# First stage of an encoder layer on one core: root sums over 128 columns, two whole and three shared early steps, the first two products by turns

## The chip, the cores and the metric

The kernel runs on one core of a Trainium2 chip. Its time is the device time of one execution, in microseconds (us). A core has five engines with a queue of instructions each: TensorE (PE in the profile; PEld is its loading of the stationary operand), VectorE (DVE), ScalarE (ACT), GpSimd (POOL) and SyncE (SP), which here only issues transfers. Each engine takes its own instructions in the order in which they stand. Data in DRAM come and go by DMA, issued on SyncE's queue or on GpSimd's.

## The reference

One layer of an encoder: 1024 tokens, width 1024. It is computed in float32.

```python
h = h + 0.5 * swiglu(rms_norm(h, ffn1_norm[l]), ffn1_w_gate[l], ffn1_w_up[l], ffn1_w_down[l])
u = rms_norm(h, mix_norm[l])
z = u @ w_in[l]
...
merged = jax.nn.sigmoid(ga) * (ya @ w_branch_a[l]) + jax.nn.sigmoid(gb) * (yb @ w_branch_b[l])
h = h + merged @ w_out[l]
h = h + 0.5 * swiglu(rms_norm(h, ffn2_norm[l]), ffn2_w_gate[l], ffn2_w_up[l], ffn2_w_down[l])
...
def rms_norm(x, g):
    xf = x.astype(jnp.float32)
    y = xf * lax.rsqrt(jnp.mean(xf * xf, axis=-1, keepdims=True) + EPS)
    return (y * g.astype(jnp.float32)).astype(x.dtype)

def swiglu(x, w_gate, w_up, w_down):
    return (jax.nn.silu(x @ w_gate) * (x @ w_up)) @ w_down
```

Between the projection `z` and `merged` stand two attentions, which the change does not touch. The feed-forward width is 2816.

## The kernel before

**Products.** Every large matrix product is done by a scheme of Strassen's kind: each operand is cut into four quadrants, and seven products of half-size operands (named P1, P2, P5, P6, P3, P7, P4, in this order) stand for eight. Each operand is split into a high and a low part (`split`, lines 86 to 89: a cast on ScalarE, a subtraction on VectorE), and `mm3` (lines 137 to 144) multiplies high by high, high by low and low by high. One product of a weight tile of 128 columns with 512 tokens is four steps of three matmuls, 128 x 128 by 128 x 512: twelve matmuls.

**The first stage**, the gate and up products of the first feed-forward, works through pairs `i` of weight tiles, 11 of them; `m` is 0 for gate and 1 for up, so a pair has 14 products. The right operands are seven combinations of the quadrants of x (transposed, tokens in the columns): B11, B21, T1, T2, B22, T3, T4 for the products P1, P2, P5, P6, P3, P7, P4. They are made on ScalarE and VectorE while TensorE works. B11 and B21 need only the first half of the tokens and the gain; T1 and all later ones need, for the second half, the ratio of the roots of the norm of the two halves. So P1 and P2 of the first five pairs are done ahead ("early", 20 products), while the sums of squares of the two halves are formed (`square`) and their roots taken (`roots`): four matmuls of the summed squares with a column of ones, the mean and the power on GpSimd, and `spread`, which lays a root out over the partitions by VectorE multiplications and four transposes. With `hidden` the first root is applied to the results just before the gate's Silu, by `units`.

**Shared and whole pairs.** In a "merged" (here: shared) pair, P1 is copied out of its PSUM bank to a buffer `u`, P2 is added to it in the bank, which gives the first quadrant, and `u` is later added to P5, P6 and P4 by VectorE. In a whole pair, P1 stays in its bank, where P6, P7 and P4 are accumulated on it, and is copied out after P1 and after P6; no `u` is needed, but the bank is held. Before the change all five early pairs are shared. Their `u` go to DRAM (`u1_d`, `store_u`, GpSimd's queue) and come back with the first quadrant when the pair's turn comes (`load_u`, SyncE's queue).

**Order.** `products` builds the list `seq` of products, `prep(q)` loads and splits the weights of product q, `prep_until` says how many are prepared ahead, and `run` is a generator that gives one step of TensorE at a time; the code around it drains so many steps between the pieces of other work. A scheduler then sets the order on each engine, except for instructions in `pin(...)`. Weights are loaded to four buffers `raw` and to two that x itself occupies at first (`extra`, tiles 6 and 7 of `fa`); intermediate results of a pair go round a `ring` of buffers in `fx` and `fa`. The small pools are `hs` (four of 512 columns) and `xs` (two of 1024). The same functions do the gate and up products of the second feed-forward, and the projection `z`, with one shared pair (i = 2); there `late_homes` places `u` in the gain's buffer and the first quadrants of pairs 2 and on in `hs`.

The early order and the lookahead of the first stage are these lines:

```python
early = [(i, p, m) for i in sorted({0, 1, *merged}) for p in ("P1", "P2") for m in range(2)]
if spill:
    early[:8] = [(i, p, m) for p in ("P1", "P2") for i in range(2) for m in range(2)]
...
prep_until(q + 3 if q < len(early) - 4 else min(2 * q - len(early) + 7, q + 8))
```

## Time and profile before

| what | us |
| --- | --- |
| median of 3 runs | 1967.34 |
| lowest, highest | 1966.22, 3939.23 |
| the profiled execution | 1967.33 |
| its span, first to last instruction | 1965.2 |

The span is what the profile's page and views cover; the other 2.1 us of that execution lie around it. In the page, the busy time of an engine is the union of its instructions, so a full TensorE reads as busy even where its clock is low; the granted clock is a column of its own (1.00 is full). A row of the timeline has start, duration, engine, line, operation, tiles written and read, shapes, count, and in brackets the idle time before it and what ended it. Consecutive matmuls overlap in the rows: their pace is the distance of the starts.

### The profile page before, as it was taken

What the parts mean: (1) busy time and instruction counts of PE and PEld (TensorE: products, weight loads), DVE (VectorE), ACT (ScalarE), POOL (GpSimd) and SP (SyncE); (2) the same over time, 40 slices, a digit from 0 to 9 for tenths busy, and PEclk for the clock granted to TensorE, in tenths of its full rate; (3) what the DMA queues carried; (4) which work ended last, traced back from release to release, by engine and by line L of the source; (5) the groups of instructions that cost most, each with busy time, mean ns of one, the idle gap of its engine ahead of it and who ended that gap; (6) DMA issues with size and microseconds to landing.
All of it is one profiled execution on the core that took longest, in us unless ns stands there. A gap on an engine that the chain in (4) does not pass through costs nothing.

```text
span 1965.2 us, 25704 instructions
## 1 busy us (share of the span) xinstructions
PE 1928.7 (98%) x8928; PEld 1601.5 (81%) x8928; DVE 1477.3 (75%) x2622; ACT 940.8 (48%) x1823; POOL 343.5 (17%) x441
## 2 busy tenths in 40 slices
PE   8999999999999999999999999999999999999998
PEld 6778888888888777888888888887888888888886
DVE  7899776668957777678878857999766556569864
ACT  6433333334446543467777873366333333344453
POOL 2011010003400112311112134500101001005100
PEclk9999999999999999999999999999999999999999
DMA  8565333367333489983358675543433332493341
GB/s 256 174 193 162 102 104 111 108 242 266 97 107 125 134 220 222 187 214 92 96 141 183 182 230 205 181 139 113 150 96 108 107 103 97 146 356 98 108 144 59
DMA packets 273873, 302.63 MB, mean 154 GB/s; under 512 B 47792, under 2 KB 200752, under 8 KB 273744
## 3 DMA queue, kind: packets, MB, share of 16 engines
q1 hardware_dynamic: 216432, 212.80, 35.4%
q0 software_dynamic: 57312, 88.20, 16.2%
q8 instruction: 70, 1.15, 0.3%
q14 instruction: 59, 0.48, 0.1%
HBM read 211.72 MB, written 89.32 MB: 153 GB/s over the span
## 4 chain that ended last, share of the span: by engine, by line
PE 75%; issue 9%; DVE 7%; DMA 4%; POOL 2%; ACT 2%; SPq 0%; POOLq 0%; DVEq 0%; ACTq 0%
PE g L140 14%; PE g L142 14%; PE g L144 14%; PE d L144 9%; PE d L140 9%; PE d L142 9%; PE d L1261 2%; DVE ws L89 1%; POOL zs_d L872 1%; PE g L1275 1%; PE d L1241 1%; PE d L1240 1%; DMA raw<-zr_d 1%; PE g L1280 1%; DMA zs_d<-hs 1%
## 5 line engine op out<-in xcount | busy, mean ns | idle before, releaser
L140 PE MATMUL g<-ar,ws 128*128 128x512 f32 x1192 | 450.1, 399 | 17.7 <-ACT ar L716 6.1
L142 PE MATMUL g<-ar,ws 128*128 128x512 f32 x1192 | 443.1, 393 | 0.1
L144 PE MATMUL g<-ar,ws 128*128 128x512 f32 x1192 | 441.3, 392 | 0.0
L89 DVE TENSOR_TENSOR ws<-raw,ws 128x512 fp32r<-128x512 f32 (+1 forms) x339 | 244.3, 725 | 167.1 <-ACT ws L88 165.2
L88 ACT CAST ws<-raw 128x512 fp32r<-128x512 f32 (+1 forms) x341 | 215.0, 638 | 279.2 <-PE d L144 114.2
L140 PEld LDWEIGHTS g<-ar,ws 128*128 128x128 f32 x1192 | 220.3, 190 | 61.7 <-ACT ar L716 6.3
L142 PEld LDWEIGHTS g<-ar,ws 128*128 128x128 f32 x1192 | 225.4, 189 | 48.7 <-DVE ar L717 1.3
L144 PEld LDWEIGHTS g<-ar,ws 128*128 128x128 f32 x1192 | 225.5, 189 | 47.9
L140 PE MATMUL d<-ar,ws 128*128 128x512 f32 x672 | 260.0, 391 | 0.9 <-ACT ws L88 0.8
L144 PE MATMUL d<-ar,ws 128*128 128x512 f32 x672 | 259.6, 390 | 1.0 <-DVE ws L89 1.0
L142 PE MATMUL d<-ar,ws 128*128 128x512 f32 x672 | 259.4, 390 | 0.0
L144 PEld LDWEIGHTS d<-ar,ws 128*128 128x128 f32 x672 | 126.4, 188 | 28.3 <-DVE ws L89 1.9
L140 PEld LDWEIGHTS d<-ar,ws 128*128 128x128 f32 x672 | 126.4, 188 | 27.8 <-ACT ws L88 1.7
L142 PEld LDWEIGHTS d<-ar,ws 128*128 128x128 f32 x672 | 126.4, 188 | 26.3
L89 DVE TENSOR_TENSOR ws<-ar,ws 128x512 fp32r<-128x512 f32 x114 | 105.9, 936 | 7.0 <-ACT ws L88 7.0
L88 ACT CAST ar<-raw 128x512 fp32r<-128x512 f32 (+1 forms) x83 | 56.0, 679 | 89.9 <-PE g L142 47.7
L413 POOL DMA_DIRECT2D hid<-fx x89 | 48.1, 540 | 287.6 <-DVE fx L474 143.7
L140 PE MATMUL g<-ws,ws 128*128 128x512 f32 x232 | 91.0, 392 | 0.1
L142 PE MATMUL g<-ws,ws 128*128 128x512 f32 x232 | 90.4, 390 | 0.0
L144 PE MATMUL g<-ws,ws 128*128 128x512 f32 x232 | 90.4, 390 | 0.0
L1248 ACT ACTIVATE fa<-fa,nmx 128x385 f32<-128x385 f32 (+3 forms) x128 | 75.6, 591 | 25.8 <-DVE nmx L1245 25.0
L89 DVE TENSOR_TENSOR ws<-fa,ws 128x512 fp32r<-128x512 f32 x74 | 51.0, 690 | 46.9 <-ACT ws L88 46.5
(312 smaller groups left out, 3535.0 us busy)
## 6 DMA issues: line engine op xcount, KB each, us to landing
raw<-hid SPq DMA_DIRECT2D x70, 512.0 KB
hid<-fx POOLq DMA_DIRECT2D x89, 256.0 KB, 2.3
raw<-in_ffn_w_up_dram SPq DMA_DIRECT2D x35, 512.0 KB
ar<-in_ffn_w_down_dram SPq DMA_DIRECT2D x32, 512.0 KB
raw<-in_ffn_w_gate_dram SPq DMA_DIRECT2D x31, 512.0 KB
raw<-in_w_in_dram SPq DMA_DIRECT2D x27, 512.0 KB
ar<-zs_d POOLq DMA_DIRECT2D x48, 256.0 KB, 5.2
hid<-fa POOLq DMA_DIRECT2D x43, 256.0 KB, 2.3
```

Source lines behind the costliest of these rows:

```text
L88: nc.scalar.copy(dst_hi, src)
L89: (eng or nc.vector).tensor_tensor(dst_lo, src, f32v(dst_hi), op=ALU.subtract)
L140: nc.tensor.matmul(b, lhs[0], r[0], start=first, stop=False, **kw)
L142: nc.tensor.matmul(b, lhs[0], r[1], start=False, stop=False, **kw)
L144: nc.tensor.matmul(b, lhs[1], r[0], start=False, stop=last, **kw)
L413: nc.gpsimd.dma_start(hid[PRODUCTS.index(p), i], src)
L872: nc.gpsimd.dma_start(dst.rearrange("p b r w -> p b (r w)"), t.rearrange("p (b k) -> p b k", b=NTT))
L1240: nc.tensor.matmul(b[:, :nw], un["q"][s], un["kd"][s][:, k0 * P:k1 * P], start=True, stop=False)
L1241: nc.tensor.matmul(b[:, :nw], un["q"][s], un["kl"][s][:, k0 * P:k1 * P], start=False, stop=True)
L1248: nc.scalar.activation(pr, pr, AF.Exp, scale=-1.0, bias=nmx[:, s:s + 1], accum_out=ssum[:, s:s + 1])
L1261: nc.tensor.transpose(pt[:, i * P:(i + 1) * P], un["pr"][s][:, i * P:(i + 1) * P], ident)
L1275: nc.tensor.matmul(o[:, s], un["v"][s][:, un["k0"] + i, :], un["p"][s][:, i], start=i == 0, stop=i == last)
```

## The change

The first stage:

- The gain column `gcol` comes by GpSimd's queue and not as the first transfer of SyncE's. The first up weights come behind the first chunk of x.
- The first two products (gate and up of pair 0, P1) run by turns, one step each, so that every chunk of x serves both.
- Pairs 0 and 1 are whole, pairs 2, 3 and 4 shared. The `u` of pairs 2 and 3 stay in the two `xs` buffers, that of pair 4 in `hs`; nothing of them goes to DRAM. The first quadrant still comes back from `hid`, where it is stored anyway. The first quadrant's product P2 of pair 0, m = 0, leaves its bank one product late (`if spill and q == 4`), when the first root is there.
- The root: four matmuls of the summed squares with a 128 x 128 matrix of 1/1024, so that 128 equal columns come out; one addition, one power on four columns. `spread` transposes the root's columns broadcast to 128 columns, without multiplications. The sums and spreads stand later in the order of products.
- Weights are prepared three products ahead up to the 26th product of this stage, and up to eight from there on; before, the lookahead grew from the 17th on.

The other two stages with `products`: u and the first quadrant of pair 2 go to the gain's buffer and to one `xs` buffer, the first quadrants of pairs 3 and on to the ring. The second half of pair 0's weights is loaded with the first half and not during the transition.

```diff
         def home(i, key, m):
-            if i < 2:
+            if i != 2:
                 return None
             if (key, m) not in homes:
-                if key == "u":
-                    u = const.tile([P, 1152], F32, tag="gain", bufs=1, name=nm_("u"))
-                    homes["u", 0], homes["u", 1] = u[:, :512], u[:, 512:1024]
-                else:
-                    homes[key, m] = main.tile([P, 512], F32, tag="hs", bufs=4, name=nm_("hs"))
+                u = const.tile([P, 1152], F32, tag="gain", bufs=1, name=nm_("u"))
+                c = xs4()
+                for k in range(2):
+                    homes["u", k], homes["11", k] = u[:, k * 512:k * 512 + 512], c[:, k * 512:k * 512 + 512]
             return homes[key, m]
...
-                if (i, m, half) not in raws and not (half and q < 4):
+                if (i, m, half) not in raws :
                     load(i, m, half)
...
-                b = bks[i]["X", m] = bank("gd"[i % 2] if spill else "d")
+                b = bks[i]["X", m] = bank("d")
...
-                b = bks[i]["X", m] = bank("g" if i == 0 else "d")
+                b = bks[i]["X", m] = bank("g" if i == 0 and not spill else "d")
...
         def run():
+            slow = len(early) + (6 if spill else -4)
             for q in range(len(seq)):
-                prep_until(q + 3 if q < len(early) - 4 else min(2 * q - len(early) + 7, q + 8))
-                yield from multiply(q)
-                i, p, m = seq[q]
...
+                prep_until(q + 3 + min(max(q - slow, 0), 5))
+                if not spill or q > 1:
+                    yield from multiply(q)
+                elif q == 0:
+                    for _ in zip(multiply(0), multiply(1)):
+                        yield
+                if spill and q == 4:
+                    continue
+                for k in ((4, 5) if spill and q == 5 else (q,)):
+                    leave(k)
...
-                for m in range(2):
-                    load(0, m, 1)
...
-                if not whole:
+                if spill and i <= merged[-1]:
                     snap["11", 1] = None
+                elif not whole:
+                    snap["11", 1] = sn()
...
     gcol = const.tile([P, NC8], F32, name="gcol")
+    nc.gpsimd.dma_start(gcol, n1c)
...
+    mean = main.tile([P, 512], F32, tag="s1", bufs=1, name=nm_("s1"))[:, :P]
+    nc.gpsimd.memset(mean, 1.0 / D)
...
     def home_1(i, key, m):
-        return main.tile([P, 512], F32, tag="hs", bufs=4, name=nm_("hs")) if i < EARLY else None
...
+        if key == "u" and i < 4:
+            if m == 0:
+                late_u[i] = xs4()
+            return late_u[i][:, m * 512:m * 512 + 512]
+        return main.tile([P, 512], F32, tag="hs", bufs=4, name=nm_("hs")) if i < 5 else None
+
+    def load_11(i, snap, sn):
+        snap["11", 0] = sn()
+        nc.sync.dma_start(snap["11", 0], hid[PRODUCTS.index("P1"), i])
+
+    hg = hidden(wg1[0], wu1[0], down.at_end, (2, 3, 4), home_1, unit, load_11, (9, 11, 1, 3, 5, 7, 0, 2, 4, 6, 8, 10))
...
-    nc.sync.dma_start(gcol, n1c)
     hg[4](0, 0, 0)
-    for c in range(4):
+    load_xq(0, 0)
+    hg[4](0, 1, 0)
+    for c in range(1, 4):
         load_xq(c, 0)
...
-            pin(nc.tensor.matmul(b[:, j:j + 1], total[:, j * P:(j + 1) * P], ones, start=True, stop=True))
+            pin(nc.tensor.matmul(b[:, j * P:(j + 1) * P], total[:, j * P:(j + 1) * P], mean, start=True, stop=True))
...
-        pin(nc.vector.tensor_scalar(ms, b[:, :4], 1.0 / D, EPS, op0=ALU.mult, op1=ALU.add))
-        for j in range(4):
-            nc.gpsimd.tensor_tensor(r[:, j:j + 1], ms[:, j:j + 1], nhalf, op=ALU.pow)
+        pin(nc.vector.tensor_scalar_add(ms, b.rearrange("p (j t) -> p j t", j=4)[:, :, 0], EPS))
+        nc.gpsimd.tensor_tensor(r, ms, nhalf4, op=ALU.pow)
...
-            pin(nc.vector.tensor_scalar_mul(w[:, j * P:(j + 1) * P], spare, cols[:, j:j + 1]))
-        return w, b, dst
...
+            pin(nc.tensor.transpose(b[:, j * P:(j + 1) * P], cols[:, j:j + 1].broadcast_to([P, P]), ident))
         pin(nc.scalar.copy(dst, b))
...
     drain(run, 4)
     r = roots(0, total)
-    w = spread(units[:, :512], r)
+    drain(run, 4)
+    spread(units[:, :512], r)
...
-    drain(run, 4)
-    spread_end(*w)
-    unit["r"] = units[:, :512]
+    drain(run, 8)
     for c in range(4, 8):
         total = square(1, c)
+    hg[3](3, place=raw4)
     drain(run, 8)
     r = roots(1, total)
-    w = spread(units[:, 512:1024], r)
+    hg[3](4, place=raw4)
     drain(run, 4)
-    spread_end(*w)
-    hg[3](3, place=raw4)
+    spread(units[:, 512:1024], r)
...
-    chunks(T1, t1, 2, -1.0)
-    hg[3](4, place=raw4)
+    drain(run, 8)
+    chunks(T1, t1, 4, -1.0)
```

How the instructions stand now is shown at three places. First ScalarE at the start of the program, before; `ws` is a split weight tile, `raw` a loaded one, `fx` a chunk of x, `ar_79` the operand B11, `ar_117` the squares, and numbers tell buffers of one name apart:

```order
L88 CAST ws_128<-raw_92 128x512
L716 ACTIVATE ar_79<-fx_75,gcol 128x512
L716 ACTIVATE ar_79<-fx_76,gcol 128x512
L716 ACTIVATE ar_79<-fx_77,gcol 128x512
L716 ACTIVATE ar_79<-fx_78,gcol 128x512
L88 CAST ws_131<-raw_98 128x512
L88 CAST ws_134<-raw_100 128x512
```

And the same place on ScalarE now; line 725 is what was line 716:

```order
L88 CAST ws_127<-raw_93 128x512
L725 ACTIVATE ar_79<-fx_75,gcol 128x512
L725 ACTIVATE ar_79<-fx_76,gcol 128x512
L88 CAST ws_130<-raw_96 128x512
L725 ACTIVATE ar_79<-fx_77,gcol 128x512
L725 ACTIVATE ar_79<-fx_78,gcol 128x512
L88 CAST ws_133<-raw_101 128x512
```

The second weight tile has moved from behind the four chunks of x to a place behind the second.

Second, TensorE at the first root, before; `g` and `d` are PSUM banks, `ar_79` and `ar_80` the operands B11 and B21, `ar_117` holds the sum of squares:

```order
L142 MATMUL d_217<-ar_79,ws_160 128x512
L144 MATMUL d_217<-ar_79,ws_160 128x512
L140 MATMUL g_137<-ar_80,ws_187 128x512
L731 MATMUL d_230<-ones,ar_117 128x1 x4
L142 MATMUL g_137<-ar_80,ws_187 128x512
```

And now; `s_11_88` is the matrix of 1/1024, line 740 the sums:

```order
L142 MATMUL d_231<-ar_80,ws_176 128x512
L144 MATMUL d_231<-ar_80,ws_176 128x512
L740 MATMUL d_244<-s_11_88,ar_118 128x128 x4
L140 MATMUL d_256<-ar_80,ws_202 128x512
L142 MATMUL d_256<-ar_80,ws_202 128x512
```

The sums stood behind the first matmul of the fifth product and stand now behind its last, eleven matmuls later, with a whole product between them and the transposes.

Third, VectorE where pair 0 ends and the weights of the second pair's P5 are prepared, before; line 717 is the last piece of T4 (`ar_426`), lines 329, 335 and 336 form the sums of weight quadrants for P5, line 89 is the low part of a split, line 464 adds P3 or P7 to what is there, lines 407 to 474 are the gate and what follows it:

```order
L717 SCALAR_TENSOR_TENSOR ar_426<-fa,ar_426 128x512
L89 TENSOR_TENSOR ws_732<-raw_624,ws_732 128x512
L424 TENSOR_TENSOR fx_76<-g_735,hs_650 128x512
L424 TENSOR_TENSOR fx_78<-g_763,hs_652 128x512
L464 TENSOR_TENSOR fx_76<-d_693,fx_76 128x512
L464 TENSOR_TENSOR fx_78<-d_716,fx_78 128x512
L407 TENSOR_TENSOR fx_76<-fx_76,units_89 128x512
L329 TENSOR_TENSOR s_100_756<-fa 128x512
L464 TENSOR_TENSOR fa<-g_735,fa 128x512
L335 TENSOR_TENSOR fa<-fa 128x512
L89 TENSOR_TENSOR ws_758<-s_100_756,ws_758 128x512
```

And now; line 726 is the last piece of T4 (`ar_532`), 327, 333 and 334 the sums for P5, 471 the additions of P3 and P7, 412 to 486 the gate and what follows it:

```order
L726 SCALAR_TENSOR_TENSOR ar_532<-fa,ar_532 128x512
L471 TENSOR_TENSOR fx_77<-d_655,fx_77 128x512
L89 TENSOR_TENSOR ws_759<-raw_566,ws_759 128x512
L476 TENSOR_TENSOR fx_76<-fx_77,fx_76 128x512
L471 TENSOR_TENSOR fa<-g_136,fa 128x512
L481 TENSOR_TENSOR fx_78<-fx_75,fx_76 128x512
L412 TENSOR_TENSOR fa<-fa,units_87 128x512
L89 TENSOR_TENSOR ws_777<-raw_596,ws_777 128x512
L327 TENSOR_TENSOR s_93_783<-fa 128x512
L471 TENSOR_TENSOR fa<-g_140,fa 128x512
L333 TENSOR_TENSOR fa<-fa 128x512
L89 TENSOR_TENSOR ws_785<-s_93_783,ws_785 128x512
```

The additions of `u` (line 424, from `hs`) are gone, and the split for pair 0's last product (`ws_777`, before `ws_732`) stands directly ahead of the second pair's P5 and no longer six rows ahead of it.

67 lines of the change are left out of this document (28 added, 39 removed).

## The prediction

> **What bounds the kernel now.** I read the page first (part 1), then busy time in stretches, then the TensorE rows in order of time for the stretches that are not full, and last the rows of ScalarE, VectorE and the DMA queues that those stretches wait for. From the page:
>
> ```profile
> span 1965.2 us, 25704 instructions
> PE 1928.7 (98%) x8928; PEld 1601.5 (81%) x8928; DVE 1477.3 (75%) x2622; ACT 940.8 (48%) x1823; POOL 343.5 (17%) x441
> ```
>
> TensorE is the bound and all idle time together is 1965.2 - 1928.7 = 36.5 us. The change leaves every large matmul in place, so it can only win some of these 36.5 us, and some time in which TensorE is busy but slow. The busy time in stretches (TensorE, weight load, VectorE, ScalarE, GpSimd, each with its count; then the granted TensorE clock, the DMA share and GB/s) shows where that is in the stage the change touches:
>
> ```profile
> 20.00:40.00 20.00, 17.72 (x73) 13.66 (x71) 13.34 (x31) 14.10 (x26) 6.24 (x11) 0.83 0.76 239
> 40.00:60.00 20.00, 19.42 (x87) 15.60 (x88) 20.00 (x34) 12.76 (x23) 3.29 (x6) 1.00 0.48 150
> 60.00:80.00 20.00, 18.74 (x82) 14.88 (x81) 17.60 (x31) 7.18 (x13) 1.62 (x3) 1.00 0.76 222
> 80.00:100.00 20.00, 18.75 (x81) 14.62 (x80) 17.16 (x29) 6.69 (x12) 0.54 (x1) 1.00 0.71 195
> 120.00:140.00 20.00, 20.00 (x89) 16.30 (x88) 19.45 (x33) 7.19 (x12) 2.85 (x6) 1.00 0.55 169
> ...
> 0.00:111.70 111.70, 52.98 (x129) 25.60 (x129) 0.97 0.68 202
> ```
>
> From 120 us on TensorE is full (x89 in 20 us); before it is not, and between 20 and 40 us the granted clock falls to 0.83. The last row counts line 140 alone, the first of the three matmuls of a step: the 129th begins at 111.70, so 128 x 3 = 384 large matmuls lie before it. The rows that show the losses (start, us, work, and the wait before it):
>
> ```profile
> 6.07 0.79 PE L140 MATMUL g<-ar,ws 128*128 128x512 f32 x1 [6.07 <-ACT ar L716]
> ...
> 12.40 0.47 PE L142 MATMUL g<-ar,ws 128*128 128x512 f32 x1
> ...
> 14.99 0.39 PE L140 MATMUL d<-ar,ws 128*128 128x512 f32 x1
> ...
> 20.43 0.39 PE L140 MATMUL g<-ar,ws 128*128 128x512 f32 x1
> 21.94 1.06 PE L731 MATMUL d<-ones,ar 128*128 128x1 f32 x8 [1.12 <-DVE ar L724]
> 22.86 0.78 PE L142 MATMUL g<-ar,ws 128*128 128x512 f32 x1
> ...
> 26.33 0.40 PE L140 MATMUL g<-ar,ws 128*128 128x512 f32 x1
> ...
> 27.03 0.60 PE L753 MATMUL d<-ident,s 128*128 128x128 f32 x4
> 27.38 0.48 PE L140 MATMUL g<-ar,ws 128*128 128x512 f32 x1
> ...
> 33.41 0.39 PE L144 MATMUL d<-ar,ws 128*128 128x512 f32 x1
> 34.95 1.02 PE L731 MATMUL d<-ones,ar 128*128 128x1 f32 x8 [1.16 <-DVE ar L724]
> 35.84 0.48 PE L140 MATMUL d<-ar,ws 128*128 128x512 f32 x1
> ...
> 39.32 0.63 PE L140 MATMUL g<-ar,ws 128*128 128x512 f32 x1
> ```
>
> A large matmul at full rate takes (20.43 - 14.99) / 24 = 0.227 us. So 384 of them take 87.1 us, and 111.70 - 87.1 = 24.6 us are lost by 111.70. They split so. The start: 13 matmuls are begun by 12.40 where 12.40 us have passed, 12.40 - 2.95 = 9.45. The first root: from 20.43 to 26.33 run 9 matmuls, 5.90 - 2.04 = 3.86. The second: from 33.41 to 39.32 run 10, 5.91 - 2.27 = 3.64. The two sets of four transposes: 27.38 - 27.03 = 0.35 each at full rate, 0.7. What is left, 24.6 - 17.65 = 6.95, call it 6.9, lies between 39 and 111 us.
>
> The root losses are more than their waits: after 22.86 eight matmuls take 3.47 us, 0.43 each. The wait of 1.12 us and the eight one-column matmuls (0.92 us to the next) leave the array nearly idle and the clock is halved for a while. [...]
>
> **The change, part by part.**
>
> *The start.* Feeding order now: first weights, first x chunk, second weights, second chunk. When they arrive is read from ScalarE, which waits for each:
>
> ```profile
> 4.34 0.62 ACT L88 CAST ws<-raw 128x512 fp32r<-128x512 f32 x1 [2.32 <-DMA raw<-in_ffn_w_gate_dram]
> ...
> 5.30 0.72 ACT L716 ACTIVATE ar<-fx,gcol 128x512 fp32r<-128x512 f32 x1 [0.34 <-DMA fx<-in_xt_dram]
> ...
> 6.83 0.72 ACT L716 ACTIVATE ar<-fx,gcol 128x512 fp32r<-128x512 f32 x1 [0.81 <-DMA fx<-in_xt_dram]
> ...
> 8.02 0.72 ACT L716 ACTIVATE ar<-fx,gcol 128x512 fp32r<-128x512 f32 x1 [0.47 <-DMA fx<-in_xt_dram]
> ...
> 9.07 0.72 ACT L716 ACTIVATE ar<-fx,gcol 128x512 fp32r<-128x512 f32 x1 [0.34 <-DMA fx<-in_xt_dram]
> ...
> 10.02 0.62 ACT L88 CAST ws<-raw 128x512 fp32r<-128x512 f32 x1 [0.22 <-DMA raw<-in_ffn_w_up_dram]
> ```
>
> Transfers of equal size land 1.0 to 1.5 us apart. Without the gain column ahead of them all come about 0.45 us sooner; the second chunk is now fourth in line and lands at about 8.02 - 0.45 = 7.6. The order of ScalarE puts the second weights' cast behind that chunk, so the cast runs at 8.3 to 8.9, and TensorE, whose first three matmuls are done by 7, stands until 8.9 for the second product. From there it has all it needs, at 0.43 us a matmul until the clock rises. If that is again at 12.40, 3 + 8 matmuls are begun: 12.4 - 2.5 = 9.9 lost instead of 9.45. If the clock rises one stretch of half rate later (3.47 us, from 22.86 to 26.33 above), 1.7 more. So -0.4 to -2.1; I take -1.0. The gain column goes by GpSimd's queue, where a store of 256 KB lands after
>
> ```profile
> hid<-fx POOLq DMA_DIRECT2D x89, 256.0 KB, 2.3
> ar<-zs_d POOLq DMA_DIRECT2D x48, 256.0 KB, 5.2
> ```
>
> 2.3 to 5.2 us. Issued at about 1 us it is there between 3.3 and 6.2. The late end would move the first three matmuls only, which then still end before 8.9: nothing.
>
> *The roots.* The sums come after the fifth product (60 matmuls) instead of one matmul after the fourth product (49): 11 x 0.227 = 2.5 us later on TensorE than the 1.1 us by which the total was late. The chain on VectorE before it grows by one split (0.6 us). So no wait is left there, 0.8 us to spare. The second root comes after ten products instead of seven and a quarter, while VectorE has some 24 operations of 0.6 us in between (14.4 us against 5 products x 2.72 = 13.6 and the sums): a wait of 0 to 1 us, I take 0. The four matmuls themselves are now 128 columns wide. Nearest row: eight pieces of one column, 0.92 us; the upper end adds eight times 128/512 of a large matmul at full rate, 0.92 + 8 x 0.057 = 1.4. I take 1.1, nearer the lower since that row is the same operands. Each stands instead of 3.86 and 3.64: 7.5 - 2.2 = 5.3 won. The transposes stay: 0. Four VectorE multiplications go for each spread, and of four powers on GpSimd one stays: the reciprocal root was waited for here,
>
> ```profile
> 25.50 0.17 DVE L737 TENSOR_SCALAR half_r<-rr 128x4 f32<-128x4 f32 x1 [2.31 <-POOL rr L735]
> ```
>
> 2.31 us for four, and is now hidden behind a whole product (2.72 us) on TensorE.
>
> *Two whole and three shared pairs.* Pairs 0 and 1 no longer add the first product: their 8 + 4 additions on VectorE go, 4 come in the early steps, and 8 copies come on ScalarE, which is busy 12.76 us of 20 at its fullest here and hides them. The ten stores of 256 KB and their reloads fall out of GpSimd's and SyncE's queues; nobody on TensorE waited for them, 0 by itself. What counts is VectorE, which from the second spread on sets the pace. Its rows:
>
> ```profile
> 41.46 0.74 DVE L757 SCALAR_TENSOR_TENSOR fx<-fx,gcol,units 128x512 f32<-128x512 f32 x1
> ...
> 90.83 0.68 DVE L717 SCALAR_TENSOR_TENSOR ar<-fa,ar 128x512 fp32r<-128x512 f32 x1
> ...
> 97.94 0.69 DVE L329 TENSOR_TENSOR s<-fa 128x512 f32<-128x512 f32 x1 [2.84 <-DMA fa<-in_ffn_w_gate_dram]
> ```
>
> Between the first use of the second spread (41.46) and the last piece of the seventh operand (90.83 + 0.68) stand 78 operations in its order: 50 us, of which 2.4 idle, so 0.61 each. After the change 70 stand there, 42.7 us. The spread itself comes at 132 x 0.227 = 29.9, plus the start 10.4, two sums 2.2, one set of transposes 0.35 and the copy 0.6 = 43.5. So the seventh operand is ready at 86.2 to 88.6, 3 to 5 us sooner. With it come free the last buffers of x, into which the next weights are loaded:
>
> ```profile
> 90.70 1.22 SPq L309 DMA_DIRECT2D fa<-in_ffn_w_gate_dram  x2
> ```
>
> The second of these starts when the seventh operand is done (91.5) and lands 6.4 us later (97.94). Now that is 92.6 to 95.0, and 1.4 us later the first matmul that needs it can start (sum, then cast), 94.0 to 96.4. In the new TensorE order this matmul stands ahead of pair 0's last product, at 348 x 0.227 = 79.0 + 10.4 + 2.2 + 0.7 = 92.3. So TensorE waits 1.7 to 4.1 us there; earlier, from the fifth products on, the splits on VectorE come within half a microsecond of their use, since weights are now prepared only three products ahead up to there: 0 to 1 us more. Against 6.9 lost before I take 3.0 lost now: 3.9 won, between 1.8 and 6.9.
>
> *Later stages.* TensorE's order there is the same, matmul for matmul. The first quadrant moves to a buffer that holds nothing at that time, the later quadrants into the ring of result buffers, the second half of the first weights is loaded sooner: 0, with TensorE full behind it. The cover would be gone where VectorE is late, as here:
>
> ```profile
> 777.48 0.77 PE L140 MATMUL g<-ar,ws 128*128 128x512 f32 x1 [2.87 <-DVE fa L894]
> ...
> 780.58 0.40 PE L142 MATMUL g<-ar,ws 128*128 128x512 f32 x1
> ```
>
> This wait costs 2.87 us, and seven matmuls behind it take 3.10 instead of 1.59: 4.4 us. It may come or go with the order of VectorE, so plus or minus 4 us for the range.
>
> The sum: -1.0 + 5.3 + 3.9 = 8.2 us off. The profiled execution took 1967.33 us (span 1965.2), as the median of the runs, 1967.34. So 1959 us, and for the terms' own ends 1955 to 1963.
>
> **The rivals.**
> - *More is won.* VectorE, with 8 operations less, is never late: nothing lost between 39 and 97 (6.9 won) and the wait at 777 goes as well (4.4). For it: the stalls end at 111 although VectorE stays over 90% busy. Against: the loads into x's buffers. 1967.3 less 11 to 15: 1952 to 1956.
> - *The late loads take most of it back.* If these land at 98 as before, since the queue ahead of them is as long, TensorE waits from 92.3 to 99.4, 7.1 us, and gets half rate, 1.7 us: 8.8 lost instead of 3.0. 1965. For it: the 2.84 us wait stands in the trace. Against: the issue moves with the seventh operand.
> - *Slower than before.* In the two later stages with this planner the first quadrants of pairs 3 and on now share the ring with the other results, and a ring buffer is free only when GpSimd's store of it has landed (2.3 to 5.2 us). If ScalarE stands at such a buffer, casts behind it are late. A wait of that kind costs what the one at 777 does, 4.4; two cancel the gain, from three on the kernel is slower: four give 1967.3 - 8.2 + 17.6 = 1977. Against: a buffer comes up again after at least eight results, more than 20 us.
> - *The turns do not work.* If the second weights land even later, the start alone loses 3 us more: 1962. The 1.7 us of one more stretch of half rate belong to this too. [...]
>
> **How the numbers follow.** Forecast 0.52 (1955 to 1963), more won 0.17, late loads 0.16, turns fail 0.07, slower 0.08. The range that leaves out no more than 2 in 10 is 1952 to 1966. A measurement of this kernel tells about 2%, 39 us, from no change. Faster by that would need more than all idle time of TensorE: 0.01. Slower by that would need nine waits like that at 777: 0.02. Within: 0.97.
>
> **What would show it.** TensorE's first wait for the second product should end near 8.9 us; no wait before the 128-column sums and a clock of 1.00 between 20 and 40 us; fewer VectorE operations up to the seventh operand, which ends near 87; one wait of 2 to 4 us near 92; the matmul with which the second pair's fourth of seven products begins (111.70 before) near 103; and the same waits as before from 600 us on. The prediction is wrong if the clock still drops after a root, if the wait near 92 is over 7 us, or if new waits stand behind 110 us.

## The result and the profile after

| | before | after |
| --- | --- | --- |
| median | 1967.12 us (4 runs) | 1954.7 us (4 runs, 1951.71 to 1955.34) |
| profiled execution, its span | 1967.33, 1965.2 us | 1954.71, 1952.9 us |

The ratio is 0.9935, with an interval of 0.9916 to 0.9955: 12.4 us less, inside the 2% band, but apart from 1. The kernel before has one run of 3939.23 us, twice the others: it is left out of the ratio but stands in the median of 1967.12, which is 1966.89 without it.

From the page of the changed kernel:

```profile
span 1952.9 us, 25648 instructions
PE 1921.4 (98%) x8928; PEld 1597.8 (82%) x8928; DVE 1473.0 (75%) x2606; ACT 944.5 (48%) x1831; POOL 337.4 (17%) x426
```

Its busy time in two of the stretches that were shown of before (same columns), and line 140 up to 104.82 us:

```profile
20.00:40.00 20.00, 19.92 (x96) 16.36 (x95) 17.60 (x32) 16.40 (x31) 2.20 (x3) 1.00 0.57 158
...
60.00:80.00 20.00, 19.70 (x87) 16.01 (x86) 19.98 (x35) 11.17 (x21) 1.08 (x2) 1.00 0.25 78
...
0.00:104.82 104.82, 52.00 (x128) 24.92 (x129) 1.00 0.60 177
```

Between 20 and 40 us the clock is 1.00 (0.83 before) and 96 matmuls begin (73 before). The 385th large matmul begins at 104.82, where it was 111.70: the first stage has won 6.88 us up to there. The other 5.6 us of the difference between the two profiled executions (12.46 us to the last large matmul) come later, where the prediction had 0.

TensorE's rows of the changed kernel for the start, the roots and the waits behind them:

```profile
5.88 0.79 PE L140 MATMUL g<-ar,ws 128*128 128x512 f32 x1 [5.88 <-ACT ar L725]
...
8.88 0.80 PE L140 MATMUL g<-ar,ws 128*128 128x512 f32 x1 [0.99 <-ACT ws L88]
...
14.19 0.40 PE L140 MATMUL g<-ar,ws 128*128 128x512 f32 x1
...
21.73 0.39 PE L140 MATMUL d<-ar,ws 128*128 128x512 f32 x1
...
24.69 1.13 PE L740 MATMUL d<-s,ar 128*128 128x128 f32 x8
25.58 0.48 PE L140 MATMUL d<-ar,ws 128*128 128x512 f32 x1
...
39.78 1.05 PE L740 MATMUL d<-s,ar 128*128 128x128 f32 x8
40.59 0.48 PE L140 MATMUL d<-ar,ws 128*128 128x512 f32 x1
...
92.50 0.47 PE L140 MATMUL g<-ar,ws 128*128 128x512 f32 x1 [0.44 <-DVE fa L471]
...
96.51 0.50 PE L140 MATMUL d<-ar,ws 128*128 128x512 f32 x1 [1.02 <-ACT ws L88]
...
122.60 0.50 PE L140 MATMUL g<-ar,ws 128*128 128x512 f32 x1 [1.29 <-DVE fx L471]
```

The second product is waited for until 8.88 (forecast 8.9). Neither set of sums has a wait in brackets, and no half rate follows. Near 92 stand two short waits. The wait at 122.60 is new: before, none of over 0.3 us stood between 108 and 600 us. Up to 200 us it and its neighbours give back 1.4 of the 6.88 us. VectorE's last piece of the seventh operand, and the first use of the weights in x's last buffers:

```profile
89.27 0.68 DVE L726 SCALAR_TENSOR_TENSOR ar<-fa,ar 128x512 fp32r<-128x512 f32 x1
...
95.11 0.69 DVE L327 TENSOR_TENSOR s<-fa 128x512 f32<-128x512 f32 x1 [0.96 <-DMA fa<-in_ffn_w_gate_dram]
```

Most of the later gain is in the projection `z`. There `hs` is also the buffer through which the attention's operands go to DRAM (`zs_d`). Before, ScalarE and VectorE stood for such a buffer until its store had landed; first ScalarE's rows, then VectorE's, of the kernel before:

```profile
749.73 0.64 ACT L866 ACTIVATE hs<-fa 128x512 fp32r<-128x512 f32 x1 [1.61 <-DMA zs_d<-hs]
756.74 0.63 ACT L866 ACTIVATE hs<-fa 128x512 fp32r<-128x512 f32 x1 [2.74 <-DMA zs_d<-hs]
...
759.98 0.69 DVE L867 SCALAR_TENSOR_TENSOR hs<-fa,hs 128x512 fp32r<-128x512 f32 x1 [5.26 <-DMA zs_d<-hs]
```

The same instructions of the changed kernel (VectorE, then TensorE at the matmul that waited 2.87 us at 777.48 before):

```profile
750.47 0.69 DVE L871 SCALAR_TENSOR_TENSOR hs<-fa,hs 128x512 fp32r<-128x512 f32 x1
...
770.28 0.39 PE L140 MATMUL g<-ar,ws 128*128 128x512 f32 x1
```

No brackets: nothing is waited for. What remains in this stage is a wait for a load, which is longer in this trace (TensorE stood 1.55 us there before):

```profile
716.54 1.23 DVE L922 TENSOR_TENSOR xs<-xs,fx 128x1024 f32<-128x1024 f32 x1 [2.95 <-DMA xs<-z_d]
...
718.43 0.50 PE L140 MATMUL g<-ar,ws 128*128 128x512 f32 x1 [2.96 <-DVE fa L900]
```

### The profile page after: what moved, and what is told of

It reads as the page before. It is cut to its first block, busy times and chain, and to the rows that moved or that the text cites. A ratio compares the mean times of both kernels' runs of the same rounds, so it can differ in the third digit from the quotient of the medians.

```text
span 1952.9 us, 25648 instructions
## 1 busy us (share of the span) xinstructions
PE 1921.4 (98%) x8928; PEld 1597.8 (82%) x8928; DVE 1473.0 (75%) x2606; ACT 944.5 (48%) x1831; POOL 337.4 (17%) x426
## 4 chain that ended last, share of the span: by engine, by line
PE 78%; issue 9%; DVE 6%; POOL 3%; DMA 2%; ACT 2%; SPq 0%; POOLq 0%; DVEq 0%; ACTq 0%
PE g L140 15%; PE g L142 15%; PE g L144 15%; PE d L140 9%; PE d L142 9%; PE d L144 9%; PE d L1265 2%; POOL zs_d L876 1%; PE g L1279 1%; DVE ws L89 1%; PE g L1284 1%; PE d L1244 1%; PE d L1245 1%; DVE ar L1390 1%; DVE ar L726 1%
## 5 line engine op out<-in xcount | busy, mean ns | idle before, releaser
L140 PE MATMUL g<-ar,ws 128*128 128x512 f32 x1160 | 435.5, 397 | 17.5 <-ACT ar L725 5.9
L142 PE MATMUL g<-ar,ws 128*128 128x512 f32 x1160 | 428.8, 392 | 0.8 <-DVE ar L89 0.4
L144 PE MATMUL g<-ar,ws 128*128 128x512 f32 x1160 | 427.5, 391 | 0.3 <-DVE ws L89 0.3
L140 PE MATMUL d<-ar,ws 128*128 128x512 f32 x704 | 272.2, 390 | 1.2 <-ACT ws L88 1.0
L144 PE MATMUL d<-ar,ws 128*128 128x512 f32 x704 | 271.4, 389 | 0.0
L142 PE MATMUL d<-ar,ws 128*128 128x512 f32 x704 | 271.3, 389 | 0.0
L140 PEld LDWEIGHTS g<-ar,ws 128*128 128x128 f32 x1160 | 213.3, 189 | 59.5 <-DVE fa L900 6.0
L144 PEld LDWEIGHTS g<-ar,ws 128*128 128x128 f32 x1160 | 218.4, 188 | 47.5 <-DVE ws L89 1.1
L142 PEld LDWEIGHTS g<-ar,ws 128*128 128x128 f32 x1160 | 218.4, 188 | 47.5 <-DVE ar L89 0.9
L140 PEld LDWEIGHTS d<-ar,ws 128*128 128x128 f32 x704 | 132.2, 188 | 29.6 <-ACT ws L88 1.8
L144 PEld LDWEIGHTS d<-ar,ws 128*128 128x128 f32 x704 | 132.1, 188 | 27.9 <-DVE ws L89 0.4
L142 PEld LDWEIGHTS d<-ar,ws 128*128 128x128 f32 x704 | 132.2, 188 | 27.1
```

Of the source, the lines that this page charges most:

```text
L140: nc.tensor.matmul(b, lhs[0], r[0], start=first, stop=False, **kw)
L142: nc.tensor.matmul(b, lhs[0], r[1], start=False, stop=False, **kw)
L144: nc.tensor.matmul(b, lhs[1], r[0], start=False, stop=last, **kw)
```

## The experiments

Theory: the first stage won by its roots and the order behind them, and the later stages because the first quadrants no longer take `hs` buffers. A scheduler sets the order again in every kernel, so an edit can move instructions far from it; where that matters it is said. Rivals stand with most runs. Ratios are to the kernel before, on the same chip. The last four columns are from each kernel's profiled execution, in us: the start of the 49th, 145th and 385th large matmul, and from the 385th to the last.

| kernel | median | ratio, interval | 49th | 145th | 385th | rest |
| --- | --- | --- | --- | --- | --- | --- |
| before | 1967.12 | 1 | 20.43 | 51.06 | 111.70 | 1844.5 |
| after | 1954.7 | 0.9935, 0.9916 to 0.9955 | 21.73 | 46.82 | 104.82 | 1839.0 |
| a_again | 1951.07 | 0.9917, 0.9905 to 0.9930 | 21.85 | 46.93 | 104.91 | 1837.0 |
| b_late_new | 1960.54 | 0.9966, 0.9954 to 0.9978 | 19.96 | 50.45 | 111.06 | 1839.2 |
| a_late_homes_old | 1955.58 | 0.9947, 0.9931 to 0.9963 | 20.31 | 45.54 | 102.26 | 1840.1 |
| b_roots_wide | 1963.4 | 0.9985, 0.9976 to 0.9993 | 20.05 | 47.01 | 108.21 | 1845.7 |
| a_narrow_sums | 1952.82 | 0.9932, 0.9917 to 0.9946 | 22.27 | 47.36 | 102.97 | 1841.8 |
| a_no_turns | 1954.07 | 0.9934, 0.9920 to 0.9948 | 19.55 | 45.04 | 102.64 | 1838.2 |
| a_cast_first | 1953.81 | 0.9937, 0.9923 to 0.9951 | 19.46 | 45.88 | 103.25 | 1837.9 |
| a_five_shared | 1953.55 | 0.9938, 0.9924 to 0.9953 | 20.81 | 46.24 | 104.39 | 1835.9 |
| a_old_lookahead | 1953.16 | 0.9933, 0.9920 to 0.9945 | 21.16 | 46.26 | 102.54 | 1836.5 |
| a_rope_later | 1952.2 | 0.9929, 0.9915 to 0.9942 | 20.57 | 45.68 | 103.47 | 1841.0 |
| a_best | 1952.86 | 0.9931, 0.9919 to 0.9944 | 19.86 | 45.21 | 102.90 | 1837.2 |

In these runs the kernel before took 1966.16, 1966.51 and 1965.01 us (one median for each group of four). The changed kernel was measured twice, 0.9935 and 0.9917. The intervals of its variants overlap with both, but for that of `a_late_homes_old`, which does not reach the second's.

**a_again**: the changed kernel, unaltered.

> The changed kernel once more, unaltered, as the measure for its variants. Both theories: 1954.7 us, within 2 us; second pair's P6 begins within 0.5 us of 104.82. What differs between its two profiles is scatter: by the theory that the later stages' gain comes from buffers, VectorE never stands more than 2 us for a landed store of zs_d and TensorE has no wait over 1 us between 760 and 780; by the theory that it is the luck of landing times, a wait of about 3 us there may well be back, and the wait of 3.1 us at 715 gone.

The first stage repeats within 0.12 us at the 145th and the 385th matmul. The wait near 716 is 1.55 us here and was 2.96, none stands near 770: the later gain is no luck of one trace.

**b_late_new**: the later stages' part alone, on the kernel before.

```diff
-            if i < 2:
+            if i != 2:
...
-                    homes[key, m] = main.tile([P, 512], F32, tag="hs", bufs=4, name=nm_("hs"))
+                c = xs4()
+                for k in range(2):
+                    homes["u", k], homes["11", k] = u[:, k * 512:k * 512 + 512], c[:, k * 512:k * 512 + 512]
...
-                for m in range(2):
-                    load(0, m, 1)
...
```

> The kernel before with only the later stages' part of the change (first quadrant of pair 2 in an xs buffer, those of pairs 3 and on in the ring, second half of the first weights with the first half). Buffer theory: before, VectorE stood 5.26 us at 759.98 for a store from hs, since the first quadrants take two of the four hs buffers; with these free the wait goes, and with it the wait of 2.87 us and the half rate at 777. 1967 - 4.5 = 1962.5 us (1961 to 1964); the first stage unchanged, second pair's P6 at 111.7. Luck theory: 1967, within 2 us, and the wait near 777 is there.

0.34% of 1966 us less, 6.7 us (4.3 to 9.0): somewhat over the 4.5 expected, and 1960.54 is just below the expected 1961 to 1964. The matmul that waited at 777.48 begins in step:

```profile
774.54 0.39 PE L140 MATMUL g<-ar,ws 128*128 128x512 f32 x1
```

The rest behind the 385th matmul is 5.3 us shorter than before, with the first stage unchanged. Counted between the same two matmuls, 4.6 us of that are the wait and its half rate. Another 1.2 us go near 1309, where VectorE held TensorE up for 0.80 us; that wait is gone in every kernel with the earlier load of the first weights and is there in `b_roots_wide`. The rest is scatter of this trace: no half rate behind the wait near 1331 (1.6 us less), a wait of 2.66 us and half rate near 1110 (2.5 us more). The luck theory falls.

**a_late_homes_old**: the reverse, the first quadrants back in `hs`.

```diff
-            if i != 2:
+            if i < 2:
...
-                c = xs4()
...
+                    homes[key, m] = main.tile([P, 512], F32, tag="hs", bufs=4, name=nm_("hs"))
...
```

> The changed kernel with the first quadrants of the later stages put back into the hs buffers (u in the gain's buffer, nothing in xs; first stage and weight loads as changed). Buffer theory: VectorE stands about 5 us for a store from hs again, TensorE about 3 us behind it near 770 and half rate for seven matmuls: 1954.7 + 4.5 = 1959 us (1958 to 1961); second pair's P6 stays at 104.8. Luck theory: 1954.7, within 2 us, with no such wait.

The time alone does not show it: 1955.58 is below the expected 1958 to 1961, 4.5 us above `a_again` but only 0.9 above the first measurement of the changed kernel, and the runs spread from 1952.39 to 1961.48. The edit has also changed VectorE's order in the first stage, whose 385th matmul begins 2.6 us sooner. The traces do show it. The wait for the store is back on VectorE, and on TensorE behind it (two views of this kernel):

```profile
751.99 0.69 DVE L870 SCALAR_TENSOR_TENSOR hs<-fa,hs 128x512 fp32r<-128x512 f32 x1 [5.36 <-DMA zs_d<-hs]
```

```profile
769.36 0.76 PE L140 MATMUL g<-ar,ws 128*128 128x512 f32 x1 [2.85 <-DVE fa L897]
```

Half rate follows up to the row at 772.48. Between the same two matmuls (those at 729.12 and 788.09 us of the kernel before) lie 58.97 us before and 58.99 here, but 54.40 in `b_late_new`, in both runs of the changed kernel and in its other seven variants in the table. Part put in, wait gone; part taken out, wait back: the `hs` buffers are shown as the cause, and the price is 4.6 us.

**b_roots_wide**: the new form of the roots at the old places, on the kernel before.

```diff
-            pin(nc.tensor.matmul(b[:, j:j + 1], total[:, j * P:(j + 1) * P], ones, start=True, stop=True))
+            pin(nc.tensor.matmul(b[:, j * P:(j + 1) * P], total[:, j * P:(j + 1) * P], mean, start=True, stop=True))
...
```

> The kernel before with the sums of squares over 128 columns, one power for four and the transposes of broadcast columns, all at the places of before (one matmul behind the fourth product, and so on). Place theory (the wait of 1.1 us ahead of the sums is what halves the clock): the waits stay, granted clock between 20 and 40 us still about 0.83, 1967 us within 1.5. Width theory (one-column matmuls leave the array idle and that halves the clock): no half rate after the sums although the waits stay, clock 1.00, 2 x 1.6 = 3 us won, 1964.

2.8 us less (1.4 to 4.7). The waits stay, yet the clock does not fall (20 to 40 us: 1.00):

```profile
21.69 1.13 PE L733 MATMUL d<-s,ar 128*128 128x128 f32 x8 [1.26 <-DVE ar L726]
22.58 0.47 PE L142 MATMUL g<-ar,ws 128*128 128x512 f32 x1
```

That speaks for the width theory as far as it goes. But `b_late_new`, whose sums still have one column, waits longer, 1.65 us, and has no half rate behind its first sums either:

```profile
22.00 1.02 PE L730 MATMUL d<-ones,ar 128*128 128x1 f32 x8 [1.65 <-DVE ar L723]
22.89 0.49 PE L142 MATMUL g<-ar,ws 128*128 128x512 f32 x1
23.21 0.40 PE L144 MATMUL g<-ar,ws 128*128 128x512 f32 x1
```

So neither the wait nor the width decides by itself; `a_probe` below was made for this.

**a_narrow_sums**: one-column sums at the new places.

```diff
-            pin(nc.tensor.matmul(b[:, j * P:(j + 1) * P], total[:, j * P:(j + 1) * P], mean, start=True, stop=True))
+            pin(nc.tensor.matmul(b[:, j:j + 1], total[:, j * P:(j + 1) * P], mean[:, :1], start=True, stop=True))
...
```

> The changed kernel with the sums of squares taken with one column again, at the changed kernel's places (no wait ahead of them). Place theory (the wait ahead of the sums lets the clock fall): nothing is waited for, so the granted clock stays 1.00 between 20 and 40 us and the time is the changed kernel's, 1951 to 1955 us; a sum still costs 0.8 to 1.1 us of TensorE. Width theory (one-column matmuls leave the array idle for the clock's measure): half rate for some eight matmuls behind one or both sums, clock 0.83 to 0.92 there, 1.6 to 3.2 us more: 1954 to 1957.

1952.82 us, and the clock stays at 1.00, as the place theory had it:

```profile
25.23 1.02 PE L740 MATMUL d<-s,ar 128*128 128x1 f32 x8
```

The row also prices the width: 1.02 us over one column, 1.05 to 1.13 over 128. It costs at most 0.1 us.

**a_no_turns**: the first two products one behind the other, and the old order of the first transfers but for the gain column.

```diff
-                if not spill or q > 1:
-                    yield from multiply(q)
-                elif q == 0:
-                    for _ in zip(multiply(0), multiply(1)):
-                        yield
+                yield from multiply(q)
...
```

> The changed kernel with the first two products one behind the other and the old order of the first transfers (gain column still on GpSimd's queue). By the prediction's term for the start the turns cost 1.0 us (0.4 to 2.1), so the fifth product begins at 19.6 to 21.3 us and not at 21.73, and the time is about 1 us less. [...]

The fifth product begins at 19.55, 2.2 us sooner, the most that the prediction's term allowed (0.4 to 2.1); with the turns unaltered it is 20.3 to 22.3 in seven profiles, so starts differ by 2 us without that edit too. 0.5 us of the gain go into a wait ahead of the first sums (0.49 us at 22.92). The time, 1954.07, cannot be told from the changed kernel's.

**a_cast_first**: the second weights' cast ahead of the second chunk.

```diff
         put_x(B11, c, xq(c, 0), gc(c))
+        if c == 0:
+            hg[1](2)
```

> The changed kernel with ScalarE's cast of the second weights ahead of the second chunk of x (one swap in its order). If the cast's place is what TensorE waited for, its wait for the second product ends at 7.2 to 7.6 us instead of 8.88, three matmuls move into the gap, the fifth product begins 0.7 to 1.7 us sooner (20.0 to 21.0 us), and the time is about 1 us less. Rival: the second weights themselves land no sooner than 7.6 us: the wait ends at 8.3 or later, the second chunk's cast moves behind them, and nothing is won.

The cast runs at 6.73 and TensorE goes from the first to the second product at 7.56 without a wait; the fifth product begins at 19.46. Then TensorE is early for the sums:

```profile
23.73 1.13 PE L740 MATMUL d<-s,ar 128*128 128x128 f32 x8 [1.39 <-DVE ar L733]
```

1.39 us of the 2.3 go there. No gain in the time.

**a_five_shared**: all five early pairs shared, `u` through DRAM, the rest as changed.

```diff
-    hg = hidden(wg1[0], wu1[0], down.at_end, (2, 3, 4), home_1, unit, load_11, (9, 11, 1, 3, 5, 7, 0, 2, 4, 6, 8, 10))
+    hg = hidden(wg1[0], wu1[0], down.at_end, (0, 1, 2, 3, 4), home_1, unit, (store_u, load_u), (9, 11, 1, 3, 5, 7, 0, 2, 4, 6, 8, 10))
...
```

> The changed kernel with all five early pairs shared again and their u sent through DRAM (starts, roots, lookahead and later stages as changed). VectorE theory (its order sets the pace from the second spread to the seventh operand): eight operations of 0.61 us more there, the seventh operand is done about 4 us later, TensorE's wait near 92 to 95 us grows by 2 to 4 us, second pair's P6 begins at 107 to 109 us instead of 104.8, and the time is 2 to 4 us more: 1954 to 1958. Transfer theory (the loads into x's last buffers and their queue set it): the ten stores and reloads make little difference, P6 within 1 us of 104.8, and no difference in the time.

The whole pairs are worth little: the seventh operand's last piece begins at 89.74 against 89.27, and the stretch from the 145th to the 385th matmul takes 58.15 us against 58.00 (60.64 before).

```profile
89.74 0.69 DVE L728 SCALAR_TENSOR_TENSOR ar<-fa,ar 128x512 fp32r<-128x512 f32 x1
```

But the run does not refute the VectorE theory, since it put back three of VectorE's operations and not eight. These are VectorE's busy time and count from the first use of the second root to the end of the seventh operand, then clock, DMA share and GB/s: before, changed, and here.

```profile
41.45:91.52 50.07, 47.67 (x80) 1.00 0.59 177
```

```profile
46.97:89.96 42.99, 42.88 (x72) 1.00 0.36 107
```

```profile
45.81:90.43 44.62, 44.59 (x75) 1.00 0.48 143
```

VectorE takes 0.60 us an operation in each and is hardly idle. The eight operations fewer of the changed kernel are not the additions of `u` (two stood in this stretch before, none now, four here), but splits of weights, line 89: 19 before, 11 now, 10 here. It is the new lookahead that keeps them out, as the next run shows. The wait at 122.60 is not there in this kernel; in the other kernels with whole pairs it is 0.3 to 1.3 us.

**a_old_lookahead**: the old rule of the lookahead.

```diff
-                prep_until(q + 3 + min(max(q - slow, 0), 5))
+                prep_until(q + 3 if q < len(early) - 4 else min(2 * q - len(early) + 7, q + 8))
...
```

> The changed kernel with the old rule of the first stage's lookahead (growing from the 17th product on and not from the 27th). Between the 145th and the 385th large matmul TensorE lost 6.2 us before, 3.6 after the change, and 3.75 with all five pairs shared, so the whole pairs are not what won there. Lookahead theory: weights prepared too early stand ahead of the pieces of x in VectorE's order; with the old rule that stretch loses 5 to 6.5 us again and second pair's P6 begins 2 to 3 us later. Rival (the order of the pieces of x, which is written in the code and stays): the stretch still loses 3 to 4 us, no difference in the time.

With this rule the loads into x's last buffers stand ahead of the code that makes the seventh operand, so here that operand is made partly of weights, this kernel does not compute the layer, and no load waits for the operand: they go out at 78.40 (87.57 in the changed kernel).

```profile
78.40 1.57 SPq L308 DMA_DIRECT2D fa<-in_ffn_w_gate_dram  x2
```

On VectorE the lookahead theory holds. From the first use of the second root stand 83 operations where the changed kernel has 72, and the seventh operand's last piece begins at 95.18 and not at 89.27:

```profile
46.13:95.87 49.74, 49.40 (x83) 1.00 0.46 132
```

```profile
95.18 0.68 DVE L725 SCALAR_TENSOR_TENSOR ar<-fa,ar 128x512 fp32r<-128x512 f32 x1
```

TensorE's stretch takes 56.28 us all the same. Since the loads do not wait for the late operand here, as they must in a kernel that computes the layer, that does not show what the lookahead is worth to TensorE. Nor do the early loads explain the 1.7 us less than in the changed kernel: `a_narrow_sums`, with the loads in their place, takes 55.61.

**a_rope_later**: the rotation's sums emitted two products behind their loads.

```diff
+        hook(14 * (NG - 1) - 8 - 3 * c, rope_sum, c)
...
```

> The changed kernel with the rotation's sums on VectorE two products behind their loads (the loads stay where they are). In the profile VectorE stood 2.95 us for such a load at 713.6 and TensorE 3.1 us behind it at 715; all other profiles have 1.7 to 3 us there. If the load's landing is the cause, the wait of VectorE and the two waits of TensorE near 711 and 715 go: 2 to 3.5 us less than the changed kernel. Rival: the late instruction behind it on VectorE is late anyway (its own queue), and TensorE waits on: 0 to 1 us.

A miss of the edit: the scheduler put the sum where it had been, ahead of the late instruction, and the wait stays.

```profile
714.83 1.22 DVE L927 TENSOR_TENSOR xs<-xs,fx 128x1024 f32<-128x1024 f32 x1 [2.47 <-DMA xs<-z_d]
715.98 0.68 DVE L900 SCALAR_TENSOR_TENSOR fa<-g,fa 128x512 f32<-128x512 f32 x1
```

Whether holding it back by a pin would win the 1.5 to 3 us was not tried.

**a_best**: `a_rope_later` and `a_no_turns` together.

> The last edit together with the first two products one behind the other (the old order of the first transfers but for the gain column). By the profiles the fifth product begins at about 19.6 instead of 21.7 us, of which a wait ahead of the first sums takes about 0.6 back: 1 to 1.5 us; with 2 to 3.5 us near 715 the sum is 3 to 5 us less than the changed kernel: 1948 us (1946.5 to 1950.5). Rival, if neither term is real: the changed kernel's 1951 to 1955.

1952.86 us and not the 1948 expected: no better than the changed kernel. None of the versions beats it measurably.

**a_probe**: sixteen gaps on TensorE in the first stage, with sums over 1 and over 128 columns by turns.

```diff
+        pin(nc.tensor.matmul(b[:, :1], ident, ident[:, :1], start=True, stop=True))
+        pin(nc.scalar.copy(rr[:, 20:21], b[:, :1]))
+        pin(nc.gpsimd.tensor_tensor(rr[:, 21:22], rr[:, 20:21], nhalf4[:, :1], op=ALU.mult))
+        for j in range(4):
+            o, s = (a[:, j * P:(j + 1) * P], ident) if k % 2 else (a[:, j:j + 1], ident[:, :1])
+            pin(nc.tensor.matmul(o, rr[:, 21:22].broadcast_to([P, P]), s, start=True, stop=True))
...
```

> The changed kernel with sixteen artificial gaps in the first stage, one about every 23 steps: a small matmul, a copy on ScalarE, a multiplication on GpSimd, and four sums that wait for it, by turns over 1 column (eight gaps) and over 128 (eight gaps); they add about 35 us. It is to show what halves the clock behind a gap. Width theory: half rate for six to eight matmuls behind most of the eight one-column gaps and behind none or one of the 128-column ones. [...]

2004.05 us, in a single run. A gap is counted from the start of the last large matmul ahead to the first one behind. Up to 2.16 us (seven gaps, three with one column and four with 128) none is followed by half rate. Of the five between 2.3 and 2.9 us two are, 2.32 and 2.85, and three are not, 2.39, 2.48 and 2.64. (Of the others, three are longer than 4.8 us, and the scheduler broke one up.) Two of the five, both with one-column sums:

```profile
300.42 1.05 PE L846 MATMUL d<-ident,rr 128*128 128x1 f32 x8 [0.89 <-POOL rr L843]
301.33 0.48 PE L143 MATMUL g<-ar,ws 128*128 128x512 f32 x1
...
302.85 0.63 PE L143 MATMUL g<-ar,ws 128*128 128x512 f32 x1
...
374.13 1.05 PE L846 MATMUL d<-ident,rr 128*128 128x1 f32 x8 [1.22 <-POOL rr L843]
375.05 0.48 PE L143 MATMUL g<-ar,ws 128*128 128x512 f32 x1
375.37 0.39 PE L145 MATMUL g<-ar,ws 128*128 128x512 f32 x1
```

The first gap (2.32 us) is punished, a microsecond and a half after it has ended (0.63 us a row instead of 0.40); the second (2.64 us) is not. So the length of a gap alone does not decide. Whether the width counts this run does not settle: only one of the five has 128 columns (2.39 us, no half rate), and two longer ones with one column (2.48 and 2.64 us) had none either. Gaps of the other kernels are in the last section.

## Why the prediction was right, and where it was not

The time, 1954.7, lies in the range of 1952 to 1966 but at its lower end: 4.3 us below 1959, and just below the 1955 to 1963 that the terms' own ends give. The terms by the two profiled executions:

| term | forecast | measured |
| --- | --- | --- |
| start (to the 49th matmul) | -1.0 (-0.4 to -2.1) | 20.43 - 21.73 = -1.3 |
| roots (49th to 145th) | +5.3 | 30.63 - 25.09 = +5.5 |
| from there to the 385th | +3.9 (1.8 to 6.9) | 60.64 - 58.00 = +2.6 |
| later stages | 0 (plus or minus 4) | 1844.5 - 1839.0 = +5.6 |

- **The start** was right, with its mechanism: the second weights' cast behind the second chunk holds TensorE until 8.88, and `a_cast_first` takes that wait away by moving the cast alone. That the number fits is in part luck, since unaltered starts differ by 2 us. What the turns cost in the end is less, since without them the sums wait.
- **The roots** were right in size. The sums cost 1.13 and 0.81 us (forecast 1.1 each; from the large matmul ahead to the one behind, less one step) and are not waited for. But the two stretches of half rate behind the old sums were taken as fixed losses; `b_late_new` has only one of them with the same sums (granted clock 0.91 between 20 and 40 us, 0.83 before). Some 1.6 us of the term for each (behind the first, eight matmuls in 3.47 us that take 1.82 at 0.227) was the luck of this one trace.
- **Between 39 and 111 us** the size was inside the range, and the working is right in part. VectorE's list is shorter by eight, as forecast, and takes 42.99 us (forecast 42.7). But the cause named, the additions of the whole pairs, is wrong: it is splits that the lookahead keeps out. The step that failed is the time at which that list begins, "and the copy 0.6 = 43.5". The transposes begin at 43.57, but the copy behind them stands on ScalarE behind a cast that waits 2.00 us for weights, and the first use is at 46.97:

```profile
45.71 0.62 ACT L88 CAST ws<-raw 128x512 fp32r<-128x512 f32 x1 [2.00 <-DMA raw<-in_ffn_w_up_dram]
46.23 0.58 ACT L756 COPY units<-d 128x512 f32<-128x512 f32 x1
```

  So the seventh operand was done at 89.95, not 86.2 to 88.6; the weights behind it landed at 95.11, at the end of 92.6 to 95.0, and the waits near 92 were 0.44 and 1.02 us, short of the 1.7 to 4.1. What won the 2.6 us on TensorE stays open. It is more than the scatter (60.6 to 61.2 us in the three kernels with the old order, 55.6 to 58.2 in the ten others of the table), and it is not the whole pairs. The lookahead, the roots' places and the order of the pieces of x are left: the change also makes the pieces of B22 and T3 by turns and those of T4 further apart, which its list does not name. None was undone by itself in a kernel that computes the layer.
- **The later stages** are the term that was mis-sized, and more than the whole of the miss: 0 forecast, 5.6 measured. Between the same matmuls of the two traces, 4.5 of it are in `z`, 1.2 near 1309, 1.2 behind the wait at 1335.88, which was followed by half rate only before, and 2.7 in shorter waits between 800 and 1290; 1.4 go back near 122, 1.3 near 715 and 1.3 near 1729. Only the first two are in every kernel with the new homes and the earlier load. The step that failed is "The first quadrant moves to a buffer that holds nothing at that time, the later quadrants into the ring of result buffers ... 0". It asked what the quadrants would find at their new place and not who waited at the old one. The trace of before had the row, 5.26 us of VectorE for a store from `hs`, 17 us ahead of the wait at 777 that the prediction quotes and leaves to "the order of VectorE".
- The rival "more is won" gave 1952 to 1956, and the time is in it, half by its reason: the wait at 777 did go, but by a buffer and not by VectorE's eight operations, and the waits between 39 and 97 did not all go. "Slower" by the ring did not happen: no such wait stands in the trace. One of the prediction's own signs of being wrong did come, a new wait behind 110 us: 1.29 us at 122.60, and 1.26 near 1729 in this trace.

## What to carry to other kernels

When a change moves a buffer, look at who else waits for the pool that it leaves: follow a wait on TensorE back through the engine it names until an idle time there ends with a transfer, and price that. A saving of one or two microseconds at the head of a stage is worth little while the next pinned step waits for another engine; here the sums took back 0.5 and 1.4 us of two savings of 2.2 and 2.3, and in the medians nothing is seen of the rest. A run that is to undo one part has to be read for what it really undid: here one put back three operations of eight, and another lost the order that makes its result right. Half rate stood behind two of the probe's five gaps between 2.3 and 2.9 us and not behind the other three: take a share of such a stretch in a forecast, and not all.

## What the runs showed of the hardware

Half rate (rows of 0.63 us, 0.43 apart) did not go by the length of the gap ahead of it. Gaps on TensorE outside the probe, counted as there, from the start of the last large matmul ahead to the start of the first one behind:

| kernel | gap | us | in it | half rate behind it |
| --- | --- | --- | --- | --- |
| before | 20.43 to 22.86 | 2.43 | sums over 1 column | yes |
| before | 33.41 to 35.84 | 2.43 | sums over 1 column | yes |
| b_late_new | 19.96 to 22.89 | 2.93 | sums over 1 column | no |
| b_roots_wide | 20.05 to 22.58 | 2.53 | sums over 128 columns | no |
| a_cast_first | 21.96 to 24.61 | 2.65 | sums over 128 columns | no |
| before | 774.22 to 777.48 | 3.26 | nothing | yes |
| a_late_homes_old | 766.12 to 769.36 | 3.24 | nothing | yes |
| after | 715.08 to 718.43 | 3.35 | nothing | no |
| before | 1333.41 to 1335.88 | 2.47 | nothing | yes |
| after | 1320.83 to 1323.32 | 2.49 | nothing | no |

The longest gap here has none behind it, and the last two, alike within 0.02 us, went both ways; first the kernel before, where rows of 0.63 us follow up to 1339.82, then the changed kernel, whose clock is 1.00 from 1323.4 to 1340:

```profile
1335.88 0.47 PE L140 MATMUL g<-ar,ws 128*128 128x512 f32 x1 [2.07 <-DVE fa L450]
...
1336.88 0.58 PE L142 MATMUL g<-ar,ws 128*128 128x512 f32 x1
```

```profile
1323.32 0.47 PE L140 MATMUL g<-ar,ws 128*128 128x512 f32 x1 [2.09 <-DVE fa L455]
1323.62 0.40 PE L142 MATMUL g<-ar,ws 128*128 128x512 f32 x1
1323.86 0.40 PE L144 MATMUL g<-ar,ws 128*128 128x512 f32 x1
```

Half rate did not always set in at once: with the first matmul at 777.48, 1.0 us behind the gap at 1336.88, and 1.5 us behind it at 302.85 in the probe.

Of these gaps and the probe's, the three with sums over 128 columns (2.39, 2.53 and 2.65 us) were not followed by half rate. With sums over one column 2.32, 2.43 (twice) and 2.85 us were, and 2.48, 2.64 and 2.93 us were not. That fits the width theory, but three gaps are few, and gaps without any sums went both ways too. What sets half rate off is not shown.
